# Decay rows loaded row by row and three heads ahead, a lighter preparation on VectorE, and the latent attention's operands loaded in parts

## The chip, the cores and the metric

The kernel runs on one core of a Trainium2 chip. The metric is the device time of one execution in microseconds (us). The profile shows five engines that work side by side: TensorE (PE, matmuls; PEld its weight loads), VectorE (DVE), ScalarE (ACT), GpSimd (POOL) and SyncE (SP, which only issues DMAs here). Each takes its instructions in order.

## What is computed

One encoder layer with three branches over 256 + 256 tokens of width 1024:

```
h = RMSNorm(x); one projection h @ w_in -> q, k, v, decay and gate logits, latents
A: conv + SiLU on q, k, v; gated delta rule, 8 heads, chunks of 64, both directions
     decay = exp(where(lower, gc[:, None] - gc[None, :], -inf)); L = (k b) k^T * decay (strict)
     T = (I + L)^-1; u = T (v b); w = T (k b exp(gc)); then chunk by chunk
     v_new = u - w S; o = q exp(gc) S + (q k^T * decay) v_new
B: multi-head latent attention, 8 heads; za = attention * silu(gate)
C: cross-attention into 256 memory tokens, 4 heads, * silu(gate)
y = x + (sum of sigmoid gate_i * (branch_i @ w_i)) @ w_out; final RMSNorm
```

Here gc is the running sum of the log decay inside a chunk, b is beta and S the state.

## The kernel before

Activations lie with features on the partitions and all 512 tokens along a row. Every fp32 product with a large weight is taken as three products of rounded halves: `weight` loads a 128x1024 tile (wr, two buffers, on SP), splits it on ScalarE (wh) and on VectorE or GpSimd (wl), and `gemm` runs 24 matmuls of 512 columns over it (tiles named gm_...).

There are three parts. The front (to some 390 us) normalises, makes the latents and decays and runs the memory and the latent attention; the latter's eight results za go to DRAM as `d_xa`. The middle (to some 812 us) runs the delta rule of branch A. The back multiplies branch A's result, merges and writes out.

In the middle, `weave` interleaves chains. Each chain yields two numbers, its cost on TensorE and how long until its next step may come, in a model's time; between steps `products` takes the next entry of the list `fill` that `plan` wrote (projections for later heads, gates `gate_tile`, gates z of the branches `z_tile`, the branches be and bm). TensorE's order is that of the model, word for word; the other engines' orders follow from priorities.

- `preps`, with `gdn_prep`: two groups of four heads. VectorE makes the decays inside blocks of 32 (tiles dr, L708, and ed, L717, with a mask on GpSimd, L721, and an exp on ScalarE, L723), then solves a triangular system column by column (tm, L778, and a sum into tt, L780), copies it (ts, L784), transposes twice (o1, o2) and copies into t32 (t, L800) and, on ScalarE, y64 (y, L807). `ready` says when the lanes may start.
- `heads_in`, with `gdn_in`: loads the decay rows e of a head (`decay_in`), masks them on GpSimd (L837), takes the exp on ScalarE (L845), and multiplies them into k k^T (kk, L879) on VectorE (na and e, L890). A head may start when it is at most two ahead of the last one finished.
- `lane(0)`, `lane(1)`, with `gdn_solve`: p (L917), yp, then for each direction two rounds of u (L967), xs (L980), us (L992), with ScalarE copying into ub, and x (L956) between.
- `heads_out`, with `gdn_out`: o (L1017), the sums of squares so (L1033), their power on GpSimd (ro, L1036), rob (L266), and the result xg.

The row table `d_r` holds the running decay sums, one row per direction, head and block, in DRAM. A head's decays need each row on 32 partitions: for each of two directions and two token halves, one DMA of 256 columns and one of 128 read four rows and repeat each 32 times.

The branch products be and bm read xe (the memory branch, from `d_xm`) and xa (the latent attention, from `d_xa`). `operand` loads such a tile on SP and puts its split right behind (L211 on ScalarE, L215 on VectorE). `load_xe` does so for four tiles, in the buffers of ts, o1, o2 and tt; `load_xa` for eight, when all heads are out.

## Time and profile before

| what | us |
|---|---|
| time, median of three runs | 957.33 (955.71 to 958.35) |
| the profiled execution | 955.18 |
| its span, first to last instruction | 953.3 |
| TensorE busy in it | 898.5 |
| VectorE / ScalarE / GpSimd busy | 598.9 / 418.2 / 205.5 |

The mean granted TensorE clock is 0.977 of full speed. In rows of groups, the numbers after the bar are the busy time, the mean length of one instruction in ns, and the idle time just before with what ended it; in a row of waits the total, how many times, and the longest; in a timeline row the start, the length, the instruction, and in brackets the idle time before it.

### The profile page before, as it was taken

To read this page: it belongs to the slowest core of one execution; us is meant where nothing else is said; L and a number is where in the kernel's file an instruction comes from. 1 tells how busy PE (TensorE), PEld (TensorE's weight loads), DVE (VectorE), ACT (ScalarE), POOL (GpSimd) and SP (SyncE) were. 2 spreads that over 40 slices of the span, in tenths; PEclk is the share of its full clock that TensorE was granted. 3 is DMA by queue.
4 is the path that set the end of the run, shared out by engine and by line. 5 is a ranking of instruction groups with operands and counts; after the bars stand their busy time and mean duration, and the time that the engine had idled before them with its cause. 6 is when DMAs were issued, how large, how long until landed. Compare 5 with 4: busy or idle time off the path is not lost.

```text
span 953.3 us, 13427 instructions
## 1 busy us (share of the span) xinstructions
PE 898.5 (94%) x5076; PEld 713.4 (75%) x5076; DVE 598.9 (63%) x1001; ACT 418.2 (44%) x754; POOL 205.5 (22%) x154
## 2 busy tenths in 40 slices
PE   6999999999999999988979989998999997999996
PEld 4877886878888788766757767776777875788885
DVE  6675447975687665758999976464525353455642
ACT  5645445555554544434363465453434342122232
POOL 4220330221123100413312223231202000222211
PEclk9999999999999999989989989998999997999999
DMA  5622312522244233353423232545333235346432
GB/s 199 224 63 87 91 59 73 159 96 82 95 141 115 77 121 106 124 169 107 155 70 111 71 118 81 177 130 168 109 91 119 89 126 184 84 151 240 122 110 89
DMA packets 52719, 114.08 MB, mean 120 GB/s; under 512 B 5680, under 2 KB 16816, under 8 KB 52656
## 3 DMA queue, kind: packets, MB, share of 16 engines
q1 hardware_dynamic: 48048, 104.85, 34.6%
q10 hardware_dynamic: 4608, 8.39, 2.4%
q8 instruction: 40, 0.66, 0.3%
q14 instruction: 23, 0.19, 0.1%
HBM read 93.03 MB, written 17.04 MB: 115 GB/s over the span
## 4 chain that ended last, share of the span: by engine, by line
PE 68%; DVE 11%; DMA 10%; issue 4%; ACT 3%; SPq 2%; POOL 1%; POOLq 0%; DVEq 0%; ACTq 0%
PE gm_qkv L230 13%; PE gm_g L230 7%; DMA e<-d_r 6%; PE gm_bg L230 5%; PE gm_za L230 5%; PE gm_bm L230 5%; PE y L1148 4%; PE gm_z L230 3%; PE gm_qm L230 2%; PE gm_be L230 2%; PE s_a L280 2%; PE gm_cq L230 2%; PE gm_qn L230 2%; PE o L1017 2%; DVE tm L778 1%
## 5 line engine op out<-in xcount | busy, mean ns | idle before, releaser
L205 POOL TENSOR_TENSOR wl_qkv<-wr_qkv,wh_qkv 128x1024 fp32r<-128x1024 f32 x24 | 60.3, 2512 | 163.9 <-ACT wh_qkv L201 77.7
L230 PE MATMUL gm_g<-hh,wh_g 128*128 128x512 f32 x192 | 54.6, 421 | 7.6 <-ACT gt_g L1075 7.5
L664 DVE SCALAR_TENSOR_TENSOR kq<-cz,prm,kq 128x510 f32<-128x510 f32 (+1 forms) x64 | 54.2, 846 | 10.3 <-ACT kq L657 9.4
L205 DVE TENSOR_TENSOR wl_g<-wr_g,wh_g 128x1024 fp32r<-128x1024 f32 x24 | 31.9, 1330 | 37.9 <-ACT wh_g L201 32.9
L230 PE MATMUL gm_qkv<-hh,wh_qkv 128*128 128x512 f32 x192 | 53.4, 411 | 0.1
L230 PE MATMUL gm_qkv<-hl,wh_qkv 128*128 128x512 f32 x192 | 53.2, 412 | 0.0
L230 PE MATMUL gm_g<-hl,wh_g 128*128 128x512 f32 x192 | 51.6, 403 | 0.0
L230 PE MATMUL gm_qkv<-hh,wl_qkv 128*128 128x512 f32 x192 | 51.3, 402 | 0.0
L230 PEld LDWEIGHTS gm_g<-hh,wh_g 128*128 128x128 f32 x192 | 37.2, 198 | 18.4 <-ACT gt_g L1075 9.3
L230 PE MATMUL gm_g<-hh,wl_g 128*128 128x512 f32 x192 | 50.6, 398 | 0.0
L845 ACT ACTIVATE e<-e,ngcl 128x256 f32<-128x256 f32 (+1 forms) x64 | 25.0, 446 | 50.4 <-POOL e L837 50.2
L230 PEld LDWEIGHTS gm_qkv<-hl,wh_qkv 128*128 128x128 f32 x192 | 36.7, 196 | 9.2 <-issue 0.9
L230 PEld LDWEIGHTS gm_g<-hl,wh_g 128*128 128x128 f32 x192 | 36.1, 191 | 9.1 <-issue 0.9
L230 PEld LDWEIGHTS gm_qkv<-hh,wl_qkv 128*128 128x128 f32 x192 | 35.9, 191 | 8.5 <-issue 0.3
L230 PEld LDWEIGHTS gm_g<-hh,wl_g 128*128 128x128 f32 x192 | 35.9, 188 | 8.5 <-issue 0.2
L837 POOL TENSOR_SCALAR_AFFINE_SELECT e<-e 128x256 f32<-128x256 f32 x32 | 14.2, 445 | 126.1 <-DMA e<-d_r 111.7
L230 PEld LDWEIGHTS gm_qkv<-hh,wh_qkv 128*128 128x128 f32 x192 | 34.9, 191 | 8.5 <-issue 0.7
L664 DVE SCALAR_TENSOR_TENSOR vf<-cz,prm,vf 128x510 f32<-128x510 f32 (+1 forms) x32 | 30.0, 936 | 16.5 <-ACT vf L657 16.2
L1118 POOL TENSOR_TENSOR mg<-mg,lg 128x512 f32<-128x512 f32 x16 | 21.6, 1348 | 85.6 <-DVE lg L1117 81.3
L1148 PE MATMUL y<-wh_wo,mh 128*128 128x512 f32 x128 | 38.9, 392 | 0.0
L201 ACT ACTIVATE wh_g<-wr_g 128x1024 fp32r<-128x1024 f32 x24 | 25.3, 1055 | 29.7 <-PE gm_g L230 14.2
L778 DVE TENSOR_TENSOR tm<-xx,tt 128x1 f32<-128x1 f32 (+30 forms) x62 | 35.6, 573 | 1.2
(388 smaller groups left out, 2254.4 us busy)
## 6 DMA issues: line engine op xcount, KB each, us to landing
wr_qkv<-in_w_dram SPq DMA_DIRECT2D x24, 512.0 KB
wr_g<-in_w_dram SPq DMA_DIRECT2D x24, 512.0 KB
wr_z<-in_w_dram SPq DMA_DIRECT2D x12, 512.0 KB
wr_za<-in_w_dram SPq DMA_DIRECT2D x8, 512.0 KB
d_g<-gt_g ACTq DMA_DIRECT2D x16, 256.0 KB
e<-d_r SPq DMA_DIRECT2D x32, 128.0 KB
wr_bm<-in_w_dram SPq DMA_DIRECT2D x8, 512.0 KB
lg<-d_g SPq DMA_DIRECT2D x16, 256.0 KB
```

The source lines that it names most:

```text
L201: nc.scalar.activation(hi[:, :n], raw[:, :n], AF.Copy)
L205: eng.tensor_tensor(lo[:, :n], raw[:, :n], hi[:, :n].bitcast(F32), op=ALU.subtract)
L230: nc.tensor.matmul(ps[:m], a[:, k * m:(k + 1) * m], xs[k][j], start=n == 0, stop=n == 3 * nk - 1)
L280: nc.tensor.matmul(sp[:, qb * 256:(qb + 1) * 256], a, b, start=j == 0, stop=j == n - 1)
L664: nc.vector.scalar_tensor_tensor(ys, zs, self.cw[:, f, m:m + 1], ys, ALU.mult, ALU.add)
L778: nc.vector.tensor_tensor(t3, xx[:, i:i + 1, 0:i].to_broadcast([P, i, i]), tt[:, 0:i, 0:i], op=ALU.mult)
L837: self.nc.gpsimd.affine_select(out=e[:, :, r], in_=e[:, :, r], pattern=[[0, 2], [sg, 128]], compare_op=ALU.is_ge, fill=NEG, base=0, channe ...
L845: self.nc.scalar.activation(e[:, s, r], e[:, s, r], AF.Exp, bias=self.ngcl[:, d, 2 * s + cch, hh:hh + 1])
L1017: nc.tensor.matmul(out, ub[:, d, s, cp], rhs, start=n == 0, stop=n == 3)
L1118: nc.gpsimd.tensor_tensor(self.merged[d], self.merged[d], gt, op=ALU.add)
L1148: nc.tensor.matmul(ps, xs[2 * j + q][a][:, t], b[:, q * 512:(q + 1) * 512], start=j == 0 and n == 0, stop=j == 3 and n == 5)
```

## The change

The row table gets a layout of one row of 2 x 384 columns per direction, head and block, written by four DMAs. `decay_in` loads each row by itself: one DMA of 768 columns onto 32 partitions, four per direction. A new chain `heads_load` issues a head's loads ahead of `heads_in`, which waits until nine units of the model's time have passed. In `gdn_prep`, dr becomes one operation, the mask is added on VectorE ahead of the matmul instead of on GpSimd behind it, and ts and t32 are copied on ScalarE. The list `fill` is put in another order, the splits of xe come after all its loads, and xa is loaded in five parts as heads finish, each split some six units later. The bm products take k = 5 to 7 last, instead of only k = 7.

```diff
@@ -225,7 +225,7 @@
-            order.sort(key=lambda o: o[1] == nk - 1)
+            order.sort(key=lambda o: o[1] >= (5 if name[1] == "m" else 7))
@@ -517,19 +517,25 @@
-                ga = self.ct("ga")[:, 0:128].rearrange("p (t h a) -> p t h a", t=2, h=8)
+                ga = self.ct("ga")[:, 0:128].rearrange("p (t c h a) -> p t c h a", t=2, c=2, h=8)
...
-                    nc.vector.tensor_tensor(
-                        ga[:, tb], g[:, 2 * s + tb, 8 * d:8 * d + 8].unsqueeze(2).to_broadcast([P, 8, 8]),
-                        anc[:, d, tb].unsqueeze(1).to_broadcast([P, 8, 8]), op=ALU.mult)
+                    for k in range(2):
+                        nc.vector.tensor_tensor(
+                            ga[:, tb, k], g[:, 2 * s + tb, 8 * d:8 * d + 8].unsqueeze(2).to_broadcast([P, 8, 4]),
+                            anc[:, d, tb, 4 * k:4 * k + 4].unsqueeze(1).to_broadcast([P, 8, 4]), op=ALU.mult)
...
-                                     ga[:, tb].rearrange("p h a -> p (h a)"),
+                                     ga[:, tb].rearrange("p c h a -> p (c h a)"),
...
-        nc.sync.dma_start(self.d_r, rs)
+        r3 = rs.rearrange("p (s i) -> p s i", s=2)
+        for d in range(2):
+            own, far = 64 * d + 32 * d, 64 * d + 32 * (1 - d)
+            nc.sync.dma_start(self.d_r[d][:, :, 0:256], r3[own:own + 32])
+            nc.sync.dma_start(self.d_r[d][:, :, 256:384], r3[far:far + 32, :, 128 * (1 - d):128 * (2 - d)])
@@ -701,27 +707,25 @@
-            rhs = self.tb(f"dr{g}{d}").rearrange("p (h t i) -> p h t i", h=4, t=4)
-            gcol = self.g[:, :, 8 * d + h0:8 * d + h0 + 4].rearrange("p t h -> p h t")
-            tri = c("trb" if d else "trf")
-            for h in range(4):
-                nc.vector.tensor_tensor(rhs[:, h], gcol[:, h].unsqueeze(2).to_broadcast([P, 4, 32]),
-                                        tri.unsqueeze(1).to_broadcast([P, 4, 32]), op=ALU.mult)
+            rhs, ed = self.tb(f"dr{g}{d}"), self.s2(f"ed{g}{d}")
+            sh = [P, 4, 4, 32]
+            def by_head(a):
+                return a[:, :, h0:h0 + 4].rearrange("p t h -> p h t").unsqueeze(3).to_broadcast(sh)
+            def by_row(a):
+                return a.unsqueeze(1).unsqueeze(1).to_broadcast(sh)
+            r4, e4 = (t.rearrange("p (h t i) -> p h t i", h=4, t=4) for t in (rhs, ed))
+            nc.vector.tensor_tensor(r4, by_head(self.g[:, :, 8 * d:8 * d + 8]), by_row(c("trb" if d else "trf")),
+                                    op=ALU.mult)
+            nc.vector.tensor_tensor(e4, by_head(self.ngcl[:, d]), by_row(c("ngb" if d else "ngf")), op=ALU.add)
...
-            nc.tensor.matmul(dp, c("bd"), rhs.rearrange("p h t i -> p (h t i)"), start=True, stop=True)
-            ed = self.s2(f"ed{g}{d}")
-            e4 = ed.rearrange("p (h t i) -> p h t i", h=4, t=4)
-            d4 = dp.rearrange("p (h t i) -> p h t i", h=4, t=4)
-            for h in range(4):
-                nc.vector.tensor_tensor(
-                    e4[:, h], d4[:, h],
-                    self.ngcl[:, d, :, h0 + h].unsqueeze(2).to_broadcast([P, 4, 32]), op=ALU.add)
-            e3 = ed.rearrange("p (w i) -> p w i", i=32)
-            nc.gpsimd.tensor_tensor(e3, e3, c("ngb" if d else "ngf").unsqueeze(1).to_broadcast([P, 16, 32]),
-                                    op=ALU.add)
+            nc.tensor.matmul(dp, c("bd"), rhs, start=True, stop=True)
+            nc.vector.tensor_tensor(ed, ed, dp, op=ALU.add)
...
-            eds.append(e3)
+            eds.append(ed.rearrange("p (w i) -> p w i", i=32))
@@ -781,7 +785,7 @@
-        nc.vector.tensor_copy(ts, tt.rearrange("p c r -> p r c"))
+        nc.scalar.activation(ts, tt.rearrange("p c r -> p r c"), AF.Copy)
@@ -797,7 +801,7 @@
-            nc.vector.tensor_copy(t32[r], (o2 if d else o1)[r, :, 16 * d:16 * d + 16].rearrange("p i u -> p u i"))
+            nc.scalar.activation(t32[r], (o2 if d else o1)[r, :, 16 * d:16 * d + 16].rearrange("p i u -> p u i"), AF.Copy)
@@ -808,21 +812,18 @@
-        self.ready[g] = self.now + (10 if g else 74)
+        self.ready[g] = self.now + (10 if g else 80)
...
-        r4 = self.d_r.rearrange("(d h c a) (s i) -> d h c a s i", d=2, h=8, c=2, s=2)
...
-            for s in range(2):
-                src = r4[d, hh, d, :, s]
-                nc.sync.dma_start(e[:, s, 0:256], src.unsqueeze(1).to_broadcast([4, 32, 256]))
-                src = r4[d, hh, 1 - d, :, s, 128 * (1 - d):128 * (1 - d) + 128]
-                nc.sync.dma_start(e[:, s, 256:384], src.unsqueeze(1).to_broadcast([4, 32, 128]))
+            for a in range(4):
+                src = self.d_r[d, 4 * hh + a:4 * hh + a + 1].rearrange("a s i -> a (s i)")
+                nc.sync.dma_start(e[32 * a:32 * a + 32].rearrange("p s i -> p (s i)"), src.to_broadcast([32, 768]))
@@ -851,8 +852,7 @@
-        es, vt = self.decay_in(hh)
-        yield 0.0, 10.0
+        es, vt = self.loads[hh]
@@ -1034,7 +1035,7 @@
-        yield 0.9, 5.0
+        yield 0.9, 7.0
@@ -1187,7 +1181,7 @@
-            self.d_r = dp.tile([P, 512], F32, name="d_r")
+            self.d_r = dp.tile([2, 32, 2, 384], F32, name="d_r")
@@ -1224,16 +1218,16 @@
-        self.xe, self.xa, A = [], [], self.A
+        self.xe, self.xa, self.xa_at, self.xa_raw, A = [], [None] * 8, {}, {}, self.A
+        xa = [(f, n) for n in range(5) for f in (self.load_xa, self.split_xa)]
...
-        ze = [(self.z_tile, C_ZE + h, self.d_xm[:, h], self.d_om[:, h]) for h in range(4)]
...
-        self.fill += g[0:14] + z[0:1] + qv(4) + z[1:2] + g[14:15] + vt[4:5] + qv(5) + z[2:3] + g[15:] + vt[5:6] + qv(6) + z[3:4]
-        self.fill += ze[0:1] + vt[6:7] + qv(7) + ze[1:3] + vt[7:] + ze[3:] + z[4:6] + xe + z[6:]
-        self.fill += [(self.load_xa,)] + be
+        self.fill += g[0:14] + z[0:1] + qv(4) + z[1:2] + ze[0:1] + g[14:15] + vt[4:5] + z[2:3] + qv(5) + ze[1:3] + g[15:] + vt[5:6]
+        self.fill += ze[3:] + qv(6) + z[3:6] + vt[6:7] + xe + qv(7) + z[6:] + [(self.split_x, self.xe)] + vt[7:]
+        self.fill += xa + be
@@ -1298,10 +1292,11 @@
+        self.loads, self.loaded, self.started = {}, {}, set()
...
-            self.weave((self.preps(), 1000), (self.heads_in(), 300), (self.lane(0), 2000), (self.lane(1), 2000),
+            self.weave((self.preps(), 1000), (self.heads_load(), 300), (self.heads_in(), 300), (self.lane(0), 2000), (self.lane(1), 2000),
@@ -1309,9 +1304,17 @@
+    def heads_load(self):
+        for h in range(8):
+            while h > self.out + 2 or h not in self.v_done:
+                yield 0.0, 1.0
+            self.loads[h] = self.decay_in(h)
+            self.loaded[h] = self.now + 9.0
+            yield 0.0, 1.0
...
-            while h // 4 not in self.cn or h > self.out + 2 or h not in self.v_done:
+            while h // 4 not in self.cn or self.now < self.loaded.get(h, 1e9):
@@ -1328,9 +1331,14 @@
-    def can(self, f):
-        return {self.load_xa: self.out == 8, self.branch: len(self.xa) == 8}.get(f, True)
+    def can(self, f, *a):
+        if f == self.load_xa:
+            return (3 in self.ub and self.pr[1], 5 in self.ub and 7 in self.hd, 6 in self.ub and 7 in self.hd,
+                    self.out > 6 and 7 in self.started, 7 in self.ub)[a[0]]
+        if f == self.split_xa:
+            return self.now > self.xa_at.get(a[0], 1e9)
+        return f != self.branch or None not in self.xa
@@ -1377,19 +1385,38 @@
-        self.xe.append(self.operand(t, self.d_xm[:, f]))
+        self.nc.sync.dma_start(t[:, 1].bitcast(F32), self.d_xm[:, f])
+        self.xe.append((t[:, 0], t[:, 1]))
...
-    def load_xa(self):
-        pg = self.pg
-        for f in range(0, 4, 2):
-            t = pg.tile([P, 2, 2, 512], F32R, tag="y64", bufs=2, name=f"xa{f}")
-            self.xa += [self.operand(t[:, k], self.d_xa[:, f + k]) for k in range(2)]
-        for f in range(4, 8):
-            t, n = ("ub", 2) if f < 6 else ("na", 3)
-            t = pg.tile([P, 2, 512], F32R, tag=t, bufs=n, name=f"xa{f}")
-            self.xa.append(self.operand(t, self.d_xa[:, f]))
+    def split_x(self, xs):
+        for hi, lo in xs:
+            self.split(lo.bitcast(F32), hi, lo, 0.5)
+        yield 0.0
+    def load_xa(self, part):
+        lo, hi = ((0, 2), (2, 3), (3, 4), (4, 5), (5, 8))[part]
+        ts = []
+        while lo + len(ts) < hi:
+            f = lo + len(ts)
+            if f in (0, 6):
+                t = self.pg.tile([P, 2, 2, 512], F32R, tag="y64", bufs=2, name=f"xa{f}")
+                ts += [t[:, 0], t[:, 1]]
+            else:
+                t, n = ("ub", 2) if f == 4 else ("na", 3)
+                ts.append(self.pg.tile([P, 2, 512], F32R, tag=t, bufs=n, name=f"xa{f}"))
+        for f, t in enumerate(ts, lo):
+            self.nc.sync.dma_start(t[:, 1].bitcast(F32), self.d_xa[:, f])
+        self.xa_at[part] = self.now + 6.0 if part < 4 else self.now
+        self.xa_raw[part] = ts, lo
+        yield 0.0
+    def split_xa(self, part):
+        ts, lo = self.xa_raw[part]
+        for f, t in enumerate(ts, lo):
+            self.xa[f] = t[:, 0], t[:, 1]
+            self.split(t[:, 1].bitcast(F32), t[:, 0], t[:, 1], 0.5)
```

TensorE, the end of the middle part: the last head's steps (u, xs, us, x of head 7 and o, so, rob of 6) and gm_be, a product of the memory branch. Before:

```order
L230 MATMUL gm_be7_7159<-xe3_6151,wl_be7_7157 128x512
L967 MATMUL u70_7182<-vs7_6756,y641_5540 64x128 x4
L1017 MATMUL o6_7189<-e60_6352,ub6_6832 128x256
...
L980 MATMUL xs70_7205<-ub7_7181,na7_6906 64x128 x4
L992 MATMUL us70_7213<-w270_7210,y641_5540 64x128 x4
L1033 MATMUL so6_7220<-cst_293,sq6_7201 128x1 x4
L956 MATMUL x7_7228<-ub7_7181,na7_6906 128x128 x4
L266 MATMUL rob6_7235<-cst_293,ro6_7225 128x128 x4
L967 MATMUL u71_7244<-vs7_6756,y641_5540 64x128 x4
L980 MATMUL xs71_7251<-ub7_7181,na7_6906 64x128 x4
L992 MATMUL us71_7259<-w271_7256,y641_5540 64x128 x4
L1017 MATMUL o7_7266<-e70_6746,ub7_7181 128x256
```

and in the changed kernel:

```order
L230 MATMUL gm_be6_7160<-xe3_5983,wh_be6_7156 128x512
L968 MATMUL u71_7165<-vs7_6511,y641_5518 64x128 x4
L230 MATMUL gm_be6_7160<-xe0_5977,wh_be6_7156 128x512
...
L230 MATMUL gm_g27_7200<-hl1_327,wh_g27_7196 128x512
L981 MATMUL xs71_7211<-ub7_6991,na7_6687 64x128 x4
L230 MATMUL gm_g27_7200<-hl2_334,wh_g27_7196 128x512
...
L266 MATMUL rob6_7243<-cst_293,ro6_7182 128x128 x4
L230 MATMUL gm_be7_7241<-xe1_5979,wh_be7_7237 128x512
...
L230 MATMUL gm_be7_7241<-xe3_5983,wh_be7_7237 128x512
L993 MATMUL us71_7255<-w271_7216,y641_5518 64x128 x4
L230 MATMUL gm_be7_7241<-xe0_5977,wh_be7_7237 128x512
...
L1018 MATMUL o7_7277<-e70_6501,ub7_6991 128x256
```

Before, these steps stood in one row behind the last be product, with nothing between them; now each lies among products of gates (gm_g27) and be, and only o7 stands alone behind the last.

SP, the loads around head 3 and 4: weights wr, decay rows e, and xe. Before:

```order
L196 DMA wr_qkv22_5274<-in_w8_dram 128x1024
L823 DMA e30_5138<-d_r_61 128x1x256
L196 DMA wr_z31_5383<-in_w8_dram 128x1024
L825 DMA e30_5138<-d_r_61 128x1x128
L823 DMA e30_5138<-d_r_61 128x1x256
L825 DMA e30_5138<-d_r_61 128x1x128
L823 DMA e31_5143<-d_r_61 128x1x256
L825 DMA e31_5143<-d_r_61 128x1x128
...
L196 DMA wr_z53_5470<-in_w8_dram 128x1024
...
L823 DMA e40_5553<-d_r_61 128x1x256
```

and in the changed kernel:

```order
L826 DMA e30_5164<-d_r_61 32x768 x4
L826 DMA e31_5169<-d_r_61 32x768 x4
L196 DMA wr_qkv6_5500<-in_w8_dram 128x1024
...
L1388 DMA xe0_5977<-d_xm_64 128x512
L196 DMA wr_qkv22_5602<-in_w8_dram 128x1024
L1388 DMA xe1_5979<-d_xm_64 128x512
...
L826 DMA e40_5388<-d_r_61 32x768 x4
L826 DMA e41_5393<-d_r_61 32x768 x4
...
L1388 DMA xe2_5981<-d_xm_64 128x512
L196 DMA wr_z31_5691<-in_w8_dram 128x1024
...
L1388 DMA xe3_5983<-d_xm_64 128x512
```

The decay rows of head 3 stood behind wr_qkv22; now head 3 stands ahead of it, xe0 to xe3 stand here too (before, they stood far later, from behind head 4's rows on), and wr_qkv22 and head 4's rows lie between them.

TensorE, the first head's solve: kk of heads 1 and 2, and p of heads 0 and 1 (p10, p11), among the products gm_z28 and gm_qkv4. Before:

```order
L879 MATMUL kk100_4407<-kh10_4347 128x512
...
L230 MATMUL gm_qkv4_4513<-hh0_321,wh_qkv4_4509 128x512
...
L917 MATMUL p10_4521<-t320_3823,na0_3946 32x32 x16
L230 MATMUL gm_qkv4_4513<-hh4_347,wh_qkv4_4509 128x512
...
L917 MATMUL p11_4554<-t320_3823,na1_4346 32x32 x16
...
L879 MATMUL kk200_4845<-kh20_4781 128x512
```

and in the changed kernel:

```order
L879 MATMUL kk100_4176<-kh10_4124 128x512
...
L879 MATMUL kk200_4525<-kh20_4475 128x512
...
L230 MATMUL gm_qkv4_4558<-hh0_321,wh_qkv4_4554 128x512
...
L879 MATMUL kk210_4584<-kh21_4479 128x512
...
L230 MATMUL gm_qkv4_4558<-hl6_362,wh_qkv4_4554 128x512
...
L917 MATMUL p10_4600<-t320_3858,na0_3906 32x32 x16
L917 MATMUL p11_4619<-t320_3858,na1_4123 32x32 x16
L230 MATMUL gm_qkv4_4558<-hh3_340,wl_qkv4_4556 128x512
```

The p of heads 0 and 1 moved from behind the fourth and ninth matmul of gm_qkv4 to one place behind its nineteenth, and the kk of head 2, which came after p, now come before it.

More of the change, by code (lines that the diff above doesn't have):

```diff
@@ L939, in gdn_solve @@
         yield 0.32, 5.5
+        self.started.add(hh)
         ub = pg.tile([P, 2, 2, 2, P], F32, tag="ub", bufs=2, name=f"ub{hh}")
@@ L1340, in products @@
             while self.fill:
-                i = next((i for i, (f, *_) in enumerate(self.fill) if self.can(f)), None)
+                i = next((i for i, (f, *_) in enumerate(self.fill) if self.can(f, *_)), None)
                 if i is None:
```

5 lines of the change are left out of this document (removed).

## The prediction

> **What bounds the kernel now.** I read the page first, then the busy time by stretches, then what each engine waits for.
>
> ```profile
> span 953.3 us, 13427 instructions
> ...
> PE 898.5 (94%) x5076; PEld 713.4 (75%) x5076; DVE 598.9 (63%) x1001; ACT 418.2 (44%) x754; POOL 205.5 (22%) x154
> ...
> DMA packets 52719, 114.08 MB, mean 120 GB/s; under 512 B 5680, under 2 KB 16816, under 8 KB 52656
> ...
> PE 68%; DVE 11%; DMA 10%; issue 4%; ACT 3%; SPq 2%; POOL 1%; POOLq 0%; DVEq 0%; ACTq 0%
> PE gm_qkv L230 13%; PE gm_g L230 7%; DMA e<-d_r 6%; PE gm_bg L230 5%; PE gm_za L230 5%; PE gm_bm L230 5%; PE y L1148 4%; PE gm_z L230 3%; PE gm_qm L230 2%; PE gm_be L230 2%; PE s_a L280 2%; PE gm_cq L230 2%; PE gm_qn L230 2%; PE o L1017 2%; DVE tm L778 1%
> ```
>
> TensorE is busy for 94% of the span, so the most that any order can win is its idle time and what the lower clock around that idle time costs. The change touches no matmul's size. But the chain gives 10% to DMA, 6% to the decay rows e alone: transfers end waits that TensorE then feels. The stretches say where (us; PE, PEld, DVE, ACT, POOL busy; granted clock; DMA):
>
> ```profile
> 390.00:420.00 30.00, 27.86 (x238) 22.37 (x238) 20.42 (x53) 14.78 (x28) 11.96 (x13) 0.94 0.50 159
> 420.00:440.00 20.00, 17.55 (x66) 13.17 (x65) 12.66 (x31) 8.26 (x16) 4.38 (x6) 0.91 0.44 146
> 440.00:480.00 40.00, 36.72 (x269) 28.22 (x267) 39.59 (x69) 12.74 (x17) 15.74 (x9) 0.96 0.38 119
> 480.00:500.00 20.00, 15.50 (x178) 11.39 (x180) 17.93 (x43) 12.31 (x21) 2.06 (x1) 0.83 0.24 80
> 500.00:540.00 40.00, 40.00 (x238) 29.29 (x235) 39.06 (x72) 18.62 (x34) 10.05 (x5) 1.00 0.31 99
> 540.00:560.00 20.00, 15.97 (x141) 12.33 (x139) 17.27 (x19) 9.08 (x20) 7.10 (x6) 0.95 0.28 95
> 560.00:600.00 40.00, 37.99 (x232) 29.78 (x233) 25.86 (x48) 23.00 (x40) 13.40 (x12) 0.94 0.35 106
> 600.00:640.00 40.00, 38.22 (x262) 29.90 (x260) 22.64 (x41) 18.58 (x38) 9.57 (x10) 1.00 0.44 134
> 640.00:680.00 40.00, 35.50 (x204) 27.09 (x204) 19.28 (x31) 17.20 (x36) 10.47 (x11) 0.91 0.48 153
> 680.00:720.00 40.00, 39.16 (x269) 29.88 (x267) 15.52 (x32) 14.80 (x32) 3.75 (x6) 1.00 0.33 109
> ...
> 784.00:812.00 28.00, 20.10 (x117) 15.49 (x118) 11.37 (x20) 8.83 (x18) 1.01 (x1) 0.82 0.49 170
> ```
>
> Length minus PE busy, summed over the eleven rows, is 33.4 us of idle. Length times (1 - clock) is 20.6 us more, an upper bound for the slow clock. So **54.0 us is all that this part holds**. VectorE is nearly full in 440 to 480 (39.59 of 40) and in 500 to 540 (39.06): it is the second limit.
>
> Who keeps TensorE waiting (view of waits, PE, then POOL, then ACT; total us, times, longest):
>
> ```profile
> PE gm_g L230 <- ACT gt_g L1075: 7.5, 3, 3.0
> ...
> PE xs L980 <- ACT ub L971: 5.5, 2, 3.0
> PE p L917 <- DVE t L800: 4.8, 3, 3.5
> PE so L1033 <- ACT vt L689: 4.0, 1, 4.0
> ...
> POOL e L837 <- DMA e<-d_r: 111.7, 26, 26.7
> ...
> ACT e L845 <- POOL e L837: 50.2, 19, 5.7
> ...
> ACT ed L723 <- POOL ed L721: 16.1, 4, 7.6
> ...
> ACT xe L211 <- DMA xe<-d_xm: 14.6, 4, 6.9
> ACT xa L211 <- DMA xa<-d_xa: 13.8, 6, 5.4
> ```
>
> TensorE's releaser is mostly ScalarE, and ScalarE is only 44% busy. It works in order, and stands at an exp of decay rows (50.2 us) behind POOL's mask, which stands behind the loads of e (111.7 us); or at a split of xe or xa behind its own load. The short copies queued behind (gt_g, vt, ub) are what TensorE needs. So the loads are the root.
>
> **The change, part by part.**
>
> *The e loads.* The tile view of e, 390 to 440 us, covers three heads:
>
> ```profile
> L823 SPq DMA_DIRECT2D e<-d_r x12: 510/720/1942, 392.1 to 421.0; - x12
> L825 SPq DMA_DIRECT2D e<-d_r x12: 510/939/1995, 392.8 to 422.2; - x12
> L837 POOL TENSOR_SCALAR_AFFINE_SELECT e<-e x12: 402/409/577, 400.0 to 430.8; 128x256 f32<-128x256 f32 x12
> ```
>
> 24 issues fill 392.1 to 422.2: 30 us, where 24 x 0.51 would be 12.2. An issue that could run in 0.51 us is held up to 2 us, and the last mask starts 8.6 us after the last issue began: the transfers are the slow part. Three heads are 24 loads of 128 or 64 KB, 2.3 MB; over 30 us that is 77 GB/s, although 390 to 420 as a whole moves 159 GB/s. The small packets tell why: with one completion packet on each engine that a DMA uses, 64 e loads on 4 engines and the 339 other DMAs on 16 make 256 + 5424 = 5680, the count on the page. The new loads have 32 rows of 3072 B outermost, no longer 4 groups of 32.
>
> The Trainium skill, "DMA: Bandwidth & Descriptors", section "Why a DMA increments its semaphore by 16 and not by 1", gives the rule: the largest number up to 16 that divides both outermost dimensions. That is 4 before, as the count bears out, and 16 after. By it the 30 us become the issue floor; without it they stay, and the sum is that of rival B.
>
> As a bound of my own: bytes and number of issues are the same, so the floor is 12.2 us for three heads (4.1 per head) and the ceiling today's 30. I take the floor plus three weight issues and a landing, 16 us, because issue was held up by transfers, not the reverse. So heads 0 to 2 are there at about 408 instead of 425 to 431.
>
> *First stretch, 390 to 480.* TensorE's three gt_g stalls come to 7.5 us, and idle in these rows is 2.14 + 2.45 + 3.28 = 7.9; clock (0.06 x 30 + 0.09 x 20 + 0.04 x 40) another 5.2. The stalls at 411 and 422 are ScalarE standing at e, and go. The third is ScalarE standing at ed behind POOL:
>
> ```profile
> 450.36 0.63 ACT L723 ACTIVATE ed<-ed 128x512 f32<-128x512 f32 x1 [3.70 <-POOL ed L721]
> 451.53 3.22 PE L230 MATMUL gm_g<-hh,wh_g 128*128 128x512 f32 x8 [2.98 <-ACT gt_g L1075]
> ```
>
> POOL's add goes, but the sum with the matmul's result still queues on a full VectorE; I leave half of it. **Gain 10 of 13.1.**
>
> *Solve and p.* Durations, from the views of the lines and of POOL's and VectorE's groups:
>
> ```profile
> L708 DVE TENSOR_TENSOR dr<-g,cst x16: 246/282/625, 277.7 to 405.4; 128x128 f32<-128x128 f32 x16
> L717 DVE TENSOR_TENSOR ed<-dp,ngcl x16: 279/281/292, 384.7 to 448.7; 128x128 f32<-128x128 f32 x16
> L784 DVE COPY ts<-tt x2: 1096/1096/1097, 478.7 to 554.0; 128x1024 f32<-128x1024 f32 x2
> L800 DVE COPY t<-o x8: 570/602/623, 482.6 to 563.0; 32x512 f32<-32x512 f32 x8
> L807 ACT ACTIVATE y<-o,cst x8: 1135/1198/1212, 481.0 to 564.2; 128x512 f32<-128x512 f32 x8
> ...
> L1029 DVE TENSOR_TENSOR sq<-sq,kq 128x512 f32<-128x512 f32 x8 | 5.5, 687 | 2.6 <-ACT sq L1026 2.6
> ...
> L205 DVE TENSOR_TENSOR wl_g<-wr_g,wh_g 128x1024 fp32r<-128x1024 f32 x5 | 7.4, 1482 | 15.4 <-ACT wh_g L201 15.3
> ```
>
> VectorE loses 16 x 0.28 twice, 2 x 1.10 and 8 x 0.60: 16.0 us. It gains 12 operations of 128x512: at four times 0.28 as a ceiling, at 0.69 (L1029, the same size in one operation) as the value, 8.2. Net -8 us over both groups. ScalarE gains 2 ts and 8 t. No row has these copies there; by L807's strided 1.20 us for 512 columns, ts is 2.4 and t at most 1.2, at least its 0.60 on VectorE. So ScalarE gains 10 to 14 us in 390 to 560, where its six rows leave 94 of 170 free; but the step ts, transpose, t lies on the path to p. In order, ts 2.4, two t, two y and a kh split (0.6) and two t make 7.8 to 10.2 us after the last column, against 6.3 before (from 478.7 to 482.6 and four t of 0.60). The column solve itself ends earlier, because VectorE stood 15.4 us behind wh_g in 390 to 440, which was ScalarE standing at e: 478.7 - 15.4 is 463.3, with 2 us for what is not regained 465, and t is done at 473 to 475. TensorE came to p at about 479.7 (first t done at 483.2, less its longest wait of 3.5); 10 us earlier, but with 15 more qkv matmuls and the 12 of head 2's kk ahead of p, at 0.3 us some 8 (811.19 below: four in 1.20), it comes there at 476 to 478. The kk were to be done anyway. So the 4.8 us wait should all but go; of the 7.9 of idle and clock in 480 to 500 I take **6**, with bounds of 0 and 7.9, since the margin is only 1 to 5 us.
>
> The heads' vs loads, moved earlier, and `ga` in 8 more small operations early in the front lie beside TensorE's front products; at 0.28 us each (L717, four times as wide) `ga` costs 2.2 us at most if that cover is missing. The d_r write issues 3 more DMAs, at 0.51 each 1.5 us of SP in the front, long before the first load at 392.1 that reads it.
>
> *540 to 600.* Idle 4.0 + 2.0, clock 1.0 + 2.4: 9.4. ScalarE's vt stood behind the exps of head 3 or 4, which now load two heads ahead. The wait for ro is POOL's and only gets two more units of distance in the plan (5 to 7). **Gain 6.**
>
> *600 to 720.* Idle 1.8 + 4.5 + 0.8 = 7.1, clock 3.6. xe is split later than loaded and xa at a distance from its load, so the 14.6 us of ScalarE at xe go. **Gain 7 of 10.7**; the x and us steps of a head that are a chain of short instructions keep theirs.
>
> *Tail.* From 784 idle is 7.9 and clock 5.0.
>
> ```profile
> 798.00 1.52 PE L980 MATMUL xs<-ub,na 64*64 64x128 f32 x8 [3.03 <-ACT ub L971]
> 797.05 0.63 ACT L211 ACTIVATE xa<-xa 128x512 fp32r<-128x512 f32 x1 [5.36 <-DMA xa<-d_xa]
> 811.19 1.20 PE L230 MATMUL gm_bm<-xa,wh_bm 128*128 128x512 f32 x4 [2.41 <-ACT xa L211]
> ```
>
> xs stood because ScalarE stood at a load of xa; afterwards the last head's steps lie between products gm_g and gm_be, and only o7 stays bare. xa5 to xa7 still load at the end: from their issue after us71 TensorE has o7 and fifteen bm products of k below 5 (4.5 us by the row at 811.19, four in 1.20) before it needs them. **Gain 10 of 12.9.**
>
> *New waits.* xe and xa loads now stand in SP's order ahead of weights and e loads, each behind the release of its tile. I charge 3 us.
>
> Sum: 10 + 6 + 6 + 7 + 10 - 3 = **36 us**. The profiled execution took 955.18 us, 1.9 more than its span of 953.3, and lies 2.1 under the median 957.33. 957.3 - 36 = 921.3: **921**.
>
> **Rivals.**
>
> *A. VectorE becomes the bound.* For: 39.59 and 39.06 of 40. If only 5 of its 15.4 idle us come back, p still waits and group 1's solve ends near 550. SP then stands at xe0 (its tile is that of ts1, written at 554.0 before, L784, and free after the transpose that reads it), with wr_qkv22 behind it. Both terms of 6 go and the first 10 halves: 19 us, **938**. Against: the idle time has one cause, which goes.
>
> *B. The rows arrive no sooner.* SP still issues 8 loads a head, and each now writes 32 partitions. Then the first 10 falls to 2, the sixes to 0 and 1, 7 to 4: 14 us, **943**. Against: an issue of 0.51 held for 2 us. The Trainium skill's "SBUF — State Buffer", section "The DMA setup-cost knee (why "@ 1 MiB" ≠ asymptote)", speaks for this rival: use 128 partitions and one large transfer, not several small ones. No row here shows a load of 32 partitions repeated from one row.
>
> *C. All of it goes:* 957.3 - 54.0 = **903**.
>
> *D. Slower: SP stands in line.* Place: xe0 to xe3 and five parts of xa, nine points where SP may stand for a tile that VectorE, ScalarE or TensorE frees. Price: two weight tiles are loaded ahead, and one product is 13% of 953 over 24 loads of gm_qkv, 5.2 us, so a stand costs nothing up to about 10 us and one for one beyond. It decides at 39 us beyond cover (the sum with its 3 taken back), 4.3 us at each of the nine; with 5 us each, 45 - 39, it is **963**. For: SP's order has wr_qkv22 behind xe0 and e4 behind xe1, and it is a model's order that the chip may not keep. Against: the tiles come from group 1's solve, which ended by 564.2 before (L807) and should end earlier.
>
> *E. Nothing of it reaches the end:* the back part is full, so a gain ahead of it can't be lost there; it would have to be A, B and D mixed, **957**.
>
> **How the numbers follow.** Forecast (909 to 931) 0.58; A 0.13; B 0.10; C 0.07; E 0.04; D 0.08. The range, 904 to 946, leaves out D, E and half of C and a little of the others. About 0.3% (2.9 us) is what a measurement of this kernel can tell from no change: faster 0.87, same 0.05, slower 0.08.
>
> **What would show it.** Right: in the changed profile e is issued in some 13 us for three heads, small packets grow by 64 x 12 = 768 for e and 3 x 16 for d_r to 6496, POOL's wait for e falls below 60 us, gm_g no longer waits for gt_g, VectorE's idle behind wl_g in 390 to 440 falls below 5 us, and idle in the last 28 us of the middle part is under 3 us. Wrong by A: p waits for t for over 3 us. By B: issues still at 1 us or more. By D: weight splits (wh, wl) that wait for wr loads, with SP issuing nothing, and TensorE behind them.

## The result, and the profile after

The changed kernel takes 909.68 us (median of 4 runs, 908.48 to 911.39), the kernel before 956.52 us beside it: a ratio of **0.951** (95% interval 0.9485 to 0.9536), 46.8 us less. The forecast was 921, in a range of 904 to 946: the sign and the main mechanism held, and the size was 11 us short.

The page of the changed kernel, the lines that answer to those of before:

```profile
span 906.6 us, 13483 instructions
...
PE 878.9 (97%) x5076; PEld 704.2 (78%) x5076; DVE 584.4 (64%) x979; ACT 431.3 (48%) x764; POOL 207.6 (23%) x150
...
DMA packets 47520, 114.03 MB, mean 126 GB/s; under 512 B 6496, under 2 KB 9696, under 8 KB 47456
...
PE 83%; DVE 5%; ACT 4%; DMA 3%; issue 2%; SPq 1%; POOL 0%; POOLq 0%; DVEq 0%; ACTq 0%
```

The span is 46.7 us shorter. TensorE runs the same 5076 matmuls in 19.6 us less busy time (898.5 to 878.9), most of which is the clock (17.2 us by the windows below); the other 27.1 us were idle time. DMA's part of the chain that ended last fell from 10% to 3%, and e is no longer in it.

The stretches of the changed kernel (us; PE, PEld, DVE, ACT, POOL busy; granted clock; DMA):

```profile
390.00:420.00 30.00, 30.00 (x254) 24.13 (x253) 25.22 (x61) 20.47 (x41) 17.30 (x20) 1.00 0.63 188
420.00:440.00 20.00, 20.00 (x206) 15.43 (x205) 18.79 (x39) 5.83 (x8) 1.30 (x1) 1.00 0.34 118
440.00:460.00 20.00, 20.00 (x87) 16.10 (x86) 19.79 (x34) 7.20 (x9) 4.73 (x2) 1.00 0.44 145
460.00:480.00 20.00, 16.32 (x125) 12.94 (x124) 15.95 (x27) 14.91 (x15) 8.32 (x4) 0.90 0.28 93
480.00:500.00 20.00, 20.00 (x163) 15.42 (x162) 16.74 (x41) 12.16 (x26) 0.00 (x0) 0.93 0.27 90
...
560.00:600.00 40.00, 37.98 (x264) 29.48 (x264) 29.03 (x50) 23.97 (x47) 15.14 (x13) 1.00 0.48 140
...
740.00:766.00 26.00, 26.00 (x145) 20.86 (x144) 11.62 (x18) 9.62 (x16) 1.01 (x1) 1.00 0.46 145
766.00:800.00 34.00, 34.00 (x156) 27.67 (x155) 14.71 (x18) 7.59 (x8) 12.70 (x7) 1.00 0.55 191
```

Only 460 to 480 (3.7 us) and 560 to 600 (2.0) still have idle time in the middle part, against 33.4 us before; the clock is below 1.00 only in 460 to 500, 3.4 us by the same product against 20.6. That is 27.7 + 17.2 = 44.9 of the 46.7 us. The waits of TensorE and of GpSimd for e, and the issue of e for the first three heads with its masks:

```profile
PE p L917 <- ACT t L804: 3.7, 2, 2.9
...
PE kk L879 <- DVE e L890: 2.0, 1, 2.0
...
POOL e L838 <- DMA e<-d_r: 17.0, 5, 6.5
...
L826 SPq DMA_DIRECT2D e<-d_r x24: 303/420/1760, 392.5 to 407.2; - x24
...
L838 POOL TENSOR_SCALAR_AFFINE_SELECT e<-e x12: 401/409/1467, 398.0 to 412.6; 128x256 f32<-128x256 f32 x12
```

gm_g's wait for gt_g, so's for vt, xs's and x's for ub are gone. GpSimd waits 17.0 us for e, not 111.7. 24 issues now take 14.7 us, not 30, and the third head's masks are over at 413, not 431.

### The profile page after: what moved, and what is told of

Read it like the earlier page. It is cut to its first block, busy times and chain, and to the rows that moved or that the text cites. A ratio compares the mean times of both kernels' runs of the same rounds, so it can differ in the third digit from the quotient of the medians.

```text
span 906.6 us, 13483 instructions
## 1 busy us (share of the span) xinstructions
PE 878.9 (97%) x5076; PEld 704.2 (78%) x5076; DVE 584.4 (64%) x979; ACT 431.3 (48%) x764; POOL 207.6 (23%) x150
## 2 busy tenths in 40 slices
DMA packets 47520, 114.03 MB, mean 126 GB/s; under 512 B 6496, under 2 KB 9696, under 8 KB 47456
## 4 chain that ended last, share of the span: by engine, by line
PE 83%; DVE 5%; ACT 4%; DMA 3%; issue 2%; SPq 1%; POOL 0%; POOLq 0%; DVEq 0%; ACTq 0%
PE gm_g L230 15%; PE gm_qkv L230 13%; PE gm_z L230 6%; PE gm_bm L230 5%; PE gm_bg L230 5%; PE gm_za L230 5%; PE y L1142 4%; PE gm_be L230 3%; PE gm_qm L230 3%; PE kk L879 2%; PE s_a L280 2%; PE o L1018 2%; PE gm_cq L230 2%; PE gm_qn L230 1%; PE oa L312 1%
## 5 line engine op out<-in xcount | busy, mean ns | idle before, releaser
L670 DVE SCALAR_TENSOR_TENSOR kq<-cz,prm,kq 128x510 f32<-128x510 f32 (+1 forms) x64 | 56.1, 876 | 10.6 <-ACT kq L663 9.7
L230 PE MATMUL gm_g<-hh,wh_g 128*128 128x512 f32 x192 | 51.6, 403 | 0.0
L230 PE MATMUL gm_qkv<-hl,wh_qkv 128*128 128x512 f32 x192 | 50.7, 399 | 0.0
L1112 POOL TENSOR_TENSOR mg<-mg,lg 128x512 f32<-128x512 f32 x16 | 29.0, 1815 | 74.9 <-DVE lg L1111 74.9
L869 POOL TENSOR_TENSOR kl<-kq,kh 128x512 fp32r<-128x512 f32 x16 | 20.7, 1293 | 102.7 <-ACT kh L867 102.7
L205 DVE TENSOR_TENSOR wl_g<-wr_g,wh_g 128x1024 fp32r<-128x1024 f32 x24 | 29.7, 1236 | 21.0 <-ACT wh_g L201 9.4
L201 ACT ACTIVATE wh_qkv<-wr_qkv 128x1024 fp32r<-128x1024 f32 x24 | 25.4, 1058 | 22.9 <-PE gm_qkv L230 6.5
L230 PE MATMUL gm_bm<-xa,wh_bm 128*128 128x512 f32 x128 | 32.6, 396 | 0.0
```

What stands on the lines that cost most here:

```text
L201: nc.scalar.activation(hi[:, :n], raw[:, :n], AF.Copy)
L205: eng.tensor_tensor(lo[:, :n], raw[:, :n], hi[:, :n].bitcast(F32), op=ALU.subtract)
L230: nc.tensor.matmul(ps[:m], a[:, k * m:(k + 1) * m], xs[k][j], start=n == 0, stop=n == 3 * nk - 1)
L670: nc.vector.scalar_tensor_tensor(ys, zs, self.cw[:, f, m:m + 1], ys, ALU.mult, ALU.add)
L869: nc.gpsimd.tensor_tensor(lo, src, hi.bitcast(F32), op=ALU.subtract)
L1112: nc.gpsimd.tensor_tensor(self.merged[d], self.merged[d], gt, op=ALU.add)
```

## The experiments

Two theories stood against each other. **Theory 1:** the loads of e are the root, because each used 4 DMA engines; faster loads end ScalarE's and GpSimd's standing. **Theory 2:** the order is the root (loads three heads ahead, the list of products, the last head among products). Eight kernels take one part out or put one in; four more follow what was left.

### The new loads alone

On the kernel before, with the order unchanged:

```diff
...
-                nc.sync.dma_start(e[:, s, 0:256], src.unsqueeze(1).to_broadcast([4, 32, 256]))
...
+                nc.sync.dma_start(e[32 * a:32 * a + 32].rearrange("p s i -> p (s i)"), src.to_broadcast([32, 768]))
```

> The kernel before with the new row table and the new loads of e alone (one row on 32 partitions at a time); order, preparation, xe and xa as before. Theory 1, the loads are the root: the waits of gm_g for gt_g, of p for t and of so for vt go, the tail from 784 us on stays; some 20 to 28 us faster than before, 929 to 937. Theory 2, the order (loads three heads ahead, the list of products, the last head among products) is the root and the faster loads alone only shift the wait: 945 to 957.

932.4 us against 955.64: **0.975** (0.9731 to 0.977), 23 us less, as theory 1 said. In its timeline of TensorE, from 390 us on, only these idle times over 1 us are left until 760, and in the windows behind them the tail is as it was:

```profile
461.31 0.47 PE L882 MATMUL kk<-kh 128*128 128x512 f32 x1 [1.08 <-DVE e L893]
474.65 0.31 PE L920 MATMUL p<-t,na 32*32 32x32 f32 x2 [5.87 <-DVE t L806]
...
549.72 1.81 PE L1036 MATMUL so<-cst,sq 128*128 128x1 f32 x8 [3.06 <-ACT vt L695]
...
764.00:792.00 28.00, 19.08 (x109) 14.89 (x108) 9.76 (x18) 6.45 (x13) 1.01 (x1) 0.82 0.43 146
```

The gt_g stalls (411, 422, 448) and all waits of 560 to 760 above half a microsecond went with the loads alone. Two waits that were expected to go did not: so's for vt is 3.06 us of 4.03, and p's grew from 3.55 to 5.87 us, since TensorE now comes to p 10.9 us earlier (468.8 for 479.7) and t only 8.6 us. The tail keeps 8.9 us of idle and a clock of 0.82: theory 1 does not reach it.

### Everything but the new loads

```diff
-            for a in range(4):
-                src = self.d_r[d, 4 * hh + a:4 * hh + a + 1].rearrange("a s i -> a (s i)")
-                nc.sync.dma_start(e[32 * a:32 * a + 32].rearrange("p s i -> p (s i)"), src.to_broadcast([32, 768]))
+            for s in range(2):
+                src = r4[d, hh, d, :, s]
+                nc.sync.dma_start(e[:, s, 0:256], src.unsqueeze(1).to_broadcast([4, 32, 256]))
...
```

> The changed kernel with the old row table and the old loads of e (four rows, each repeated 32 times, in one DMA); everything else of the change kept, the earlier issue too. Theory 1: ScalarE and GpSimd stand at e again in the first stretch, and the heads' products behind; 928 to 940, POOL's wait for e above 60 us. Theory 2: within 5 us of the changed kernel, 908 to 915.

921.86 us (ratio to before 0.9641, 0.9625 to 0.9658): between the two expectations, with a wait of GpSimd for e of 56.3 us, just under the 60 of theory 1. Without the loads 12.2 us are lost, and the rest of the change alone gains 33.8. Neither theory holds alone: 23 and 34 make 57, and both together give 47, so some 10 us are stalls that either removes. The stretch from 600 to 720 is such a place: it held 7.1 us of idle before, 0.5 with the loads alone and 0.9 here, and its clock went from 0.91 in its worst window to 1.00 both times.

### The new loads on four engines

This kernel keeps the number of loads, their bytes, rows and place. Only the outermost dimension of the source is 4 instead of 32:

```diff
-                nc.sync.dma_start(e[32 * a:32 * a + 32].rearrange("p s i -> p (s i)"), src.to_broadcast([32, 768]))
+                nc.sync.dma_start(e[32 * a:32 * a + 32].rearrange("p s i -> p (s i)"), src.unsqueeze(0).to_broadcast([4, 8, 768]))
```

> The changed kernel with its loads of e kept in number, bytes and row length, but the source written as 4 groups of 8 repeats, so that a DMA is spread over 4 engines instead of 16 if the outermost dimensions decide it (small packets then 6496 - 768 = 5728). If the spread over engines is what counts: issues of the first three heads take 20 us or more instead of 15, and the time lies half way back, 915 to 930. If the row length or the number of packets counts: as the changed kernel, 908 to 912, with issues of 15 us.

921.77 us (0.9639, 0.9619 to 0.9658), the time of the kernel with the old loads within 0.1 us. The page and the tile view of e in this kernel:

```profile
DMA packets 46752, 114.02 MB, mean 124 GB/s; under 512 B 5728, under 2 KB 8928, under 8 KB 46688
...
L826 SPq DMA_DIRECT2D e<-d_r x24: 600/601/739, 391.0 to 416.7; - x24
...
L838 POOL TENSOR_SCALAR_AFFINE_SELECT e<-e x12: 401/407/662, 398.1 to 426.6; 128x256 f32<-128x256 f32 x12
```

5728 small packets are the 6496 less 64 x 12, as forecast from four engines per load, and 24 issues take 25.7 us instead of 14.7. So the whole worth of the new loads, 12 us in this kernel, is the spread over engines; the longer rows (3072 B instead of 1024 and 512, a quarter as many) bring nothing measurable by themselves. The rule of the Trainium skill ("DMA: Bandwidth & Descriptors", "Why a DMA increments its semaphore by 16 and not by 1") on how many engines a DMA gets is borne out here by count and by time.

### Without the chain that loads ahead

The chain `heads_load` is taken out of `weave`, and `heads_in` issues the loads:

```diff
...
-            while h // 4 not in self.cn or self.now < self.loaded.get(h, 1e9):
+            while h // 4 not in self.cn or h > self.out + 2 or h not in self.v_done:
                 yield 0.0, 1.0
+            self.loads[h] = self.decay_in(h)
+            yield 0.0, 10.0
```

> The changed kernel without the chain that loads ahead: a head's rows are issued when heads_in comes to it, and ten units of the model's time later it goes on, as before the change. If the loads over 16 engines are short enough, the head start is worth little: 908 to 914, POOL's wait for e up to 40 us. If the distance is what counts, 918 to 930 with GpSimd and ScalarE standing at e.

924.83 us (0.9656, 0.9632 to 0.9679), 15.2 us slower than the changed kernel. The time is in the second range, but the place is not the one I named. Its window at the end of the middle part, idle times of TensorE there, and two of ScalarE:

```profile
752.00:782.00 30.00, 22.15 (x113) 17.29 (x113) 10.21 (x19) 8.18 (x18) 2.02 (x2) 0.72 0.37 133
...
755.84 1.05 PE L981 MATMUL xs<-ub,na 64*64 64x128 f32 x8 [1.54 <-ACT ub L972]
...
758.18 1.47 PE L1034 MATMUL so<-cst,sq 128*128 128x1 f32 x8 [1.29 <-DVE sq L1030]
...
778.31 1.15 PE L1034 MATMUL so<-cst,sq 128*128 128x1 f32 x8 [2.20 <-DVE sq L1030]
...
754.76 0.63 ACT L211 ACTIVATE xa<-xa 128x512 fp32r<-128x512 f32 x1 [2.40 <-DMA xa<-d_xa]
...
770.63 0.63 ACT L211 ACTIVATE xa<-xa 128x512 fp32r<-128x512 f32 x1 [3.62 <-DMA xa<-d_xa]
```

GpSimd does wait for e more, and ScalarE a little behind it:

```profile
POOL e L838 <- DMA e<-d_r: 90.8, 11, 23.8
...
ACT e L846 <- POOL e L838: 9.7, 5, 4.4
```

But ScalarE's 9.7 us are no more than a fifth of the 50.2 of before, and most of the loss is the tail: 7.8 us of idle and a clock of 0.72 over 30 us, another 8.4. In this kernel's order all steps of the last head (u70 to o7) stand behind the last be product again. I read it so: the ten units before each head lengthen the heads' chain in the plan, the list of products runs out before the heads do, and the last head is bare. No view shows the plan's own times. What loading ahead buys, here, is where the last head lies.

### The old preparation, and the old list

The first puts the four-part dr and ed and GpSimd's mask back (ed and the mask are shown):

```diff
...
-            nc.vector.tensor_tensor(ed, ed, dp, op=ALU.add)
+            for h in range(4):
+                nc.vector.tensor_tensor(
+                    e4[:, h], d4[:, h],
+                    self.ngcl[:, d, :, h0 + h].unsqueeze(2).to_broadcast([P, 4, 32]), op=ALU.add)
...
+            nc.gpsimd.tensor_tensor(e3, e3, c("ngb" if d else "ngf").unsqueeze(1).to_broadcast([P, 16, 32]),
+                                    op=ALU.add)
```

> The changed kernel with dr and ed made as before (four operations each, the mask added on GpSimd behind the matmul). If VectorE and ScalarE's wait for ed bound the first solve: gm_g waits for gt_g again for 2 to 3 us near 450 and p waits longer, 2 to 6 us slower, 912 to 916. If there is slack: 908 to 911.

916.51 us (0.9564, 0.9536 to 0.9592), 6.8 slower, a little more than expected. gm_g did not wait again; the price showed at p and behind it (timeline of TensorE in this kernel):

```profile
480.27 0.32 PE L919 MATMUL p<-t,na 32*32 32x32 f32 x4 [4.74 <-ACT t L806]
...
558.50 1.51 PE L983 MATMUL xs<-ub,na 64*64 64x128 f32 x8 [3.70 <-ACT ub L974]
```

p's largest wait grew from 2.9 to 4.7 us: the work taken from VectorE lay in front of the column solve. Which of the three parts counts, dr, ed or the mask, was not tried.

The second puts the old `fill` back, with xe's splits right behind its loads:

```diff
-        self.fill += g[0:14] + z[0:1] + qv(4) + z[1:2] + ze[0:1] + g[14:15] + vt[4:5] + z[2:3] + qv(5) + ze[1:3] + g[15:] + vt[5:6]
-        self.fill += ze[3:] + qv(6) + z[3:6] + vt[6:7] + xe + qv(7) + z[6:] + [(self.split_x, self.xe)] + vt[7:]
+        self.fill += g[0:14] + z[0:1] + qv(4) + z[1:2] + g[14:15] + vt[4:5] + qv(5) + z[2:3] + g[15:] + vt[5:6] + qv(6) + z[3:4]
+        self.fill += ze[0:1] + vt[6:7] + qv(7) + ze[1:3] + vt[7:] + ze[3:] + z[4:6] + xe + [(self.split_x, self.xe)] + z[6:]
```

> The changed kernel with the list of products in its old order (xe's splits right behind its loads). If the loads and the parts of xa did the work: within 4 us, 908 to 914. If the order of the list fills the waits: 915 to 930, with waits of so, x or xs for ScalarE in the second half of the middle part.

922.75 us (0.9627, 0.9599 to 0.9656), 13.1 slower, though the last head is still among products. Two waits of nearly 4 us come in. They were expected behind ScalarE; each is behind VectorE, the second behind o7, where so7 now stands bare:

```profile
572.95 0.76 PE L879 MATMUL kk<-kh 128*128 128x512 f32 x1 [3.96 <-DVE e L890]
...
775.72 1.17 PE L1034 MATMUL so<-cst,sq 128*128 128x1 f32 x8 [3.88 <-DVE sq L1030]
```

The run puts back the order and the place of xe's splits together, so the 13.1 us are the worth of both.

### xa at the end: an edit that changed nothing

```diff
-            return (3 in self.ub and self.pr[1], 5 in self.ub and 7 in self.hd, 6 in self.ub and 7 in self.hd,
-                    self.out > 6 and 7 in self.started, 7 in self.ub)[a[0]]
+            return self.out == 8
...
-        self.xa_at[part] = self.now + 6.0 if part < 4 else self.now
+        self.xa_at[part] = self.now
```

> The changed kernel, but all eight tiles of xa are loaded and split only when every head is out, as before the change; the list and the rest stay. Theory 1a, the loads of xa in ScalarE's and SP's order are what the tail waited for: ScalarE stands at xa again and the first bm products behind it, 8 to 14 us slower, 918 to 924, with the idle in the last 28 us of the middle part. Theory 1b, the last head's steps lying among be products is what filled the tail: 910 to 915.

910.72 us (0.9503, 0.9475 to 0.9532), as the changed kernel. It does not tell the two readings apart: TensorE's order is the same, and SP's issues of xa stand where they stood, 2 us later. SP's timeline in this kernel, and then in the changed one (first and last row of xa):

```profile
630.45 0.80 SPq L1409 DMA_DIRECT2D xa<-d_xa  x2
...
761.92 0.91 SPq L1409 DMA_DIRECT2D xa<-d_xa  x2
```

```profile
628.32 0.80 SPq L1410 DMA_DIRECT2D xa<-d_xa  x2
...
759.61 0.91 SPq L1410 DMA_DIRECT2D xa<-d_xa  x2
```

When the loops write the load down does not set when SP issues it; the order of the engines other than TensorE comes from priorities and from which tile comes free. The new choice of tiles for xa was kept in this run. What that choice is worth was not tried.

### The copies, and p further back

Two things were left at 460 to 500: p's wait, and ScalarE's long copies in front of it. One edit puts ts and t32 back on VectorE:

```diff
-        nc.scalar.activation(ts, tt.rearrange("p c r -> p r c"), AF.Copy)
+        nc.vector.tensor_copy(ts, tt.rearrange("p c r -> p r c"))
...
-            nc.scalar.activation(t32[r], (o2 if d else o1)[r, :, 16 * d:16 * d + 16].rearrange("p i u -> p u i"), AF.Copy)
+            nc.vector.tensor_copy(t32[r], (o2 if d else o1)[r, :, 16 * d:16 * d + 16].rearrange("p i u -> p u i"))
```

> The changed kernel with the copies ts and t32 back on VectorE. If VectorE is the second limit: its column solve is not shorter, its windows at 440 to 460 and 520 to 540 are full and the copies come on top, 1 to 4 us slower, 911 to 914. If the path from the last column to p is what counts (7.8 to 10.2 us on ScalarE against 6.3): the wait of p for t falls from 3.7 us to under 1, 2 to 4 us faster, 906 to 908.

906.93 us (0.9485, 0.9459 to 0.9512). The time is the one expected of the path, but it did not come that way: p's wait for t is 3.9 us in this run, not under 1. The other edit plans the first solve three units later, which puts p ten matmuls back:

```diff
-        self.ready[g] = self.now + (10 if g else 80)
+        self.ready[g] = self.now + (10 if g else 83)
```

All four cases then ran on one chip:

> The changed kernel once more, as the measure for the three beside it on the same chip: 908 to 912.

> The kernel with ts and t32 on VectorE once more (906.9 against 909.7 of the changed kernel, in different calls). If the copies' place is worth something, 2 to 4 us under f0; if it was the spread between calls, within 1.5 us of f0.

> The changed kernel with the first solve planned 3 units later (80 to 83): p stands ten matmuls of a projection further back in TensorE's order, and the last head's us and rob come out behind the last be product. If only p's wait counts: it falls from 3.7 to about 1 us, 2 to 5 us under f0 with the clock. If the distance is just moved to the tail: us and rob wait there for 1 to 3 us, and the time is within 2 us of f0.

> Both: ts and t32 on VectorE and p ten matmuls later. If both waits at p are the same one, no more than the better of f1 and f2; if they add, 4 to 7 us under f0.

| us, median (ratio to before, interval) | p as in the change | p ten matmuls back |
|---|---|---|
| copies on ScalarE | 909.69 (0.951, 0.9489 to 0.9531) | 911.1 (0.9528, 0.9506 to 0.9551) |
| copies on VectorE | 906.83 (0.9478, 0.9456 to 0.9499) | 908.0 (0.9492, 0.9473 to 0.9511) |

With the copies on VectorE the time is 2.9 and 3.1 us lower in this table, and 2.8 in the calls before; over the eight runs of each kernel the means are 909.8 and 906.9. The step back comes out 1.4 and 1.2 us slower, which is within the spread of the single runs; a gain it is not. The views of the two lines, first on ScalarE (changed kernel), then on VectorE (on the common chip, with p's wait and the path to it), and last the same window in the first run with the copies on VectorE:

```profile
L788 ACT ACTIVATE ts<-tt x2: 2163/2165/2167, 467.8 to 546.8; 128x1024 f32<-128x1024 f32 x2
...
L804 ACT ACTIVATE t<-o x8: 1063/1118/1147, 469.8 to 556.2; 32x512 f32<-32x512 f32 x8
```

```profile
L788 DVE COPY ts<-tt x2: 1129/1798/2468, 468.2 to 546.4; 128x1024 f32<-128x1024 f32 x2
...
L804 DVE COPY t<-o x8: 543/596/640, 473.5 to 554.2; 32x512 f32<-32x512 f32 x8
...
PE p L917 <- DVE t L804: 3.9, 3, 2.4
...
465.88 1.14 DVE L784 TENSOR_REDUCE tt<-tm 128x31 f32<-128x961 f32 x1
...
476.14 1.21 DVE L804 COPY t<-o 32x512 f32<-32x512 f32 x2
...
460.00:500.00 40.00, 36.06 (x290) 28.21 (x289) 37.58 (x74) 21.70 (x36) 8.31 (x4) 0.96 0.25 83
```

```profile
460.00:500.00 40.00, 36.15 (x287) 28.20 (x286) 37.59 (x76) 21.27 (x35) 7.65 (x4) 0.91 0.26 92
```

A copy takes ScalarE about twice as long. Yet the path is no shorter on VectorE: from the end of the last column to the end of the last t it takes 10.3 us (467.0 to 477.4), and on ScalarE 10.1 (467.1 to 477.2). On VectorE the copies stand in line with the transposes and with the multiplications of other heads' decays, and the first ts copy took 2.47 us (see the last section). The idle time in 460 to 500 is the same too (3.9 against 3.7 us). The clock there does not explain the gain either: two runs of this one kernel, with the same two waits of 1.1 and 2.4 us at p, show 0.96 and 0.91. So where the 2.9 us come from stays open.

With p further back, p's wait falls to 1.5 us and the clock to nothing lost in 460 to 500, but x waits 2.3 us for ub near 565 (0.8 in the changed kernel beside it), us71 and rob6 come out behind the last be product, and so7 waits:

```profile
763.40 1.05 PE L1034 MATMUL so<-cst,sq 128*128 128x1 f32 x8 [2.52 <-DVE sq L1030]
```

The kernel with the copies on VectorE is the fastest of those run, 906.8 us.

## Why the prediction was right, and where it was short

*The root and the loads.* Right. Small packets 6496, to the packet; the issue of three heads 14.7 us for a forecast of some 13; GpSimd's wait 17.0 for under 60; VectorE's idle behind wl_g in 390 to 440 2.0 for under 5. Four engines in the place of 16 took the whole of it back. Rival B (no sooner) fell with this; its mark, issues still at 1 us or more, did not show (median 0.42).

*The sum.* Its terms against the changed kernel's windows, idle and clock together:

| stretch before | there | forecast gain | measured gain |
|---|---|---|---|
| 390 to 480 | 13.1 | 10 | 13.1 |
| 480 to 500, p | 7.9 | 6 | 0.8 |
| 540 to 600 | 9.4 | 6 | 7.4 |
| 600 to 720 | 10.7 | 7 | 10.7 |
| 784 to 812 | 12.9 | 10 | 12.9 |
| new waits | | -3 | 0 |
| sum | 54.0 | 36 | 44.9 |

The measured gain is what was there less what the windows at 460 to 500 (3.7 + 3.4) and 560 to 600 (2.0) still hold. All terms but p's were too small: I left 22 to 36% of each stretch for waits that would stay, and of all these only 2.0 us, at kk, were left. For 600 to 720 the reason was off as well. I named ScalarE's stand at xe; with the new loads alone ScalarE still stands there for 11.1 us (14.6 before), and the stretch has 0.5 us of idle left, at the old order of the list:

```profile
ACT xe L211 <- DMA xe<-d_xm: 11.1, 3, 6.1
```

So the stand at xe by itself did not make that loss; it took the late rows of e beside it. The 3 us charged for SP never came. Rival D's mark, wh or wl waiting for wr while SP issues nothing, does not show: from 390 to 800 no split waits for a load of wr, and TensorE waits for no split.

*The p term was too high.* It rested on TensorE coming to p at 476 to 478 with t done at 473 to 475. The timelines of VectorE, ScalarE and TensorE in the changed kernel:

```profile
465.95 1.14 DVE L784 TENSOR_REDUCE tt<-tm 128x31 f32<-128x961 f32 x1
...
467.77 2.17 ACT L788 ACTIVATE ts<-tt 128x1024 f32<-128x1024 f32 x1
...
474.99 2.18 ACT L804 ACTIVATE t<-o 32x512 f32<-32x512 f32 x2
...
476.14 0.32 PE L917 MATMUL p<-t,na 32*32 32x32 f32 x4 [2.91 <-ACT t L804]
```

TensorE was there at 473.2 (476.14 less 2.9), since the first stretch gave 13 us and not 10, and t was done only at 477.2: 10.1 us after the last column, inside the 7.8 to 10.2 reckoned, but that column ended at 467.1 rather than 465. The margin of 1 to 5 us was thus one of -4. So the wait of 4.8 us became one of 3.7, and the clock of 0.83 one of 0.90. Rival A's mark, p waiting for t for over 3 us, did show by the total (two waits, the longest 2.9 us); its time, 938, did not.

*The preparation.* I priced it as 8 us less of VectorE and gave it no term of its own. Undone, it costs 6.8 us: rival A's concern, that VectorE is the bound until 480, is right for the one path to p, which gave 0.8 of its 6 us; the two other terms that A would have cut, at 390 to 480 and at 540 to 600, came in full.

*The tail.* Right in place and in sign, but the cause that my row named, ScalarE's stand at xa, is at most a part. In the changed kernel ScalarE still waits 12.3 us for loads of xa (13.8 before; the longest 2.8 for 5.4), and TensorE does not feel it, since products lie there. In the kernel with the new xa and no loading ahead the last head is bare, and idle (7.8 us) and clock are back. Of that idle, 2.5 us (1.54 at xs and 0.95 at o) are waits for a ub copy right behind a stand at xa; the rest is behind VectorE and other copies. So bare steps lose time without xa too, and how much of the 12.9 us was xa's stays open. Whether xa's early parts alone would have helped bare steps was not tried.

*The forecast as a whole.* 921 stood for 36 us; rival C, all of it gone, 903. The result, 909.7, lies between them, at the edge of the forecast's own range of 909 to 931.

## What to carry to other kernels

A repeated load whose outermost dimension is 4 keeps one DMA on four engines, and 12 us of this kernel hung on that: count the small packets of the page to see it. When TensorE waits for an engine that is half idle, look at what stands first in that engine's order, and give each wait of a chain a product to lie under; how long the other chains run in the plan decides whether there is one left at the end. Moving a copy to another engine changes its length and its place in line together: here the fuller VectorE did it in half the time, and the path that it lies on came out no shorter.
